# A planned hybrid-decoder step: freed buffers to the first in line, one group for linear outputs, split x, padded small products, a shorter Newton step

## The chip, the cores and the metric

The kernel runs on one core of one Trainium2 chip. The metric is the device time of one execution in microseconds (us); the median of three runs is the kernel's time. Engines are named as in the profile: PE (TensorE), DVE (VectorE), ACT (ScalarE), POOL (GpSimd) and SP (SyncE, which issues most DMAs).

## The reference

One layer of a decoder with two mixers side by side, for a prompt of 512 tokens and eight single new tokens of running sequences, with 1024 features.

```python
h = jnp.einsum('btd,de->bte', x, w_in)
qa, ka, va, za, ga, qb, kb, vb, gb = jnp.split(h, split_points, axis=-1)
log_a = log_sigmoid(za @ w_alpha2 + b_alpha) / GATE_TEMP
o_a, s_new = gla_chunked(qa, ka, va, log_a, s0, chunk)
o_a = o_a * rsqrt(mean(o_a ** 2) + RMS_EPS) * gla_norm_g
o_b = dilated_attention(qb, k_all, v_all, q_idx, rel_bias)
mix = concatenate([o_a * silu(ga), o_b * silu(gb)])
x_new = layer_norm(DEEPNORM_ALPHA * x + mix @ w_out, ln_g, ln_b)
```

Mixer a is gated linear attention (4 heads, a decayed state of 64 by 128 each); mixer b has 8 heads that look back in three strides with a bias table `rel_bias` of 32 buckets by 8 heads. The outputs are x_new for prompt and new tokens, the states, and new rows of keys and values.

## The kernel before, in words

**The products.** Tokens are columns: xT has 1024 rows in 8 k-tiles of 128 and 520 columns (256 prompt tokens, the 8 new ones, 256 prompt tokens), in two halves u of 264 and 256 columns (`TS`). Each float32 operand is split into a high part and a rest (`split`: ACT casts `hi`, DVE subtracts to get `lo`). Each product is three matmuls, high by high, weight's high by x's rest, weight's rest by x's high (`three` and `halves`). In the trace both parts of x are called `xx` and the weights `hi_ka`, `lo_ka` and so on.

**The order of the main products.** `dense()` is one generator that issues warm-up matmuls, then the input projection group by group: ka, the gate's low-rank product (`ps_za`, then `zT` on DVE and `ps_z`), qa, qb, kb, vb, gb, va, ga, and then the output projection (`ps_yf`, `ps_y`). For ka it goes over k-tiles as they arrive: for each k, each half u and each of two weight tiles, `three`. `first_loads` issues the DMAs of x and the ka weights in the order of the list FIRST, then constants, rel_bias into `rb_raw`, and adds `weight_loads`; `first_splits` splits what has landed and marks "xs" and "kas", for which `dense` waits with `At`.

**Around it** stand generators of the mixers. `scores` gives ps_s for a pair of heads and 128 queries; the softmax runs on DVE (`pr`, `ms`) and ACT; PE transposes `pr` into `ps_pt`, ACT casts it to `pth`, DVE takes the rest `ptl`; `weighted` multiplies into `ps_pv`. `gla_state` makes chunk states (`ps_kv`, `st_all`), `gla_out(u)` the outputs of two chunks in two banks (`ps_oa`): eight products of `att` by `va` with 128 rows, then products of the queries `qa` by a state with 64 rows. `gla_head` takes a chunk's outputs through the squares `sq`, `rmss` and the scaling of `oa`. `sample_softmax` handles logits of the new tokens (`ps_sl`, `ps_pn`), `sample_gla` their linear attention (`o_r`, `ps_ort`). `residual_sample` normalises the new tokens with two small products (`ps_ms`, `ps_vs`), and `norm(t)` a tile of 128 prompt tokens. `rsqrt` is Ln and Exp on ACT with a Newton step; with `between` (in `norm`) the whole step runs on ACT.

**What sets the order.** All generators are tasks of a `Plan` with a priority (small is first). A task yields an instruction (`Op`, or a `Batch` that is issued as one), a wish for a buffer (`Need`, several at once as `Pair`) or a mark to wait for (`At`). `Plan.run` repeats: it goes over the tasks in the order of priority, `advance`s each up to its next instruction, and chooses the one whose modelled start is earliest. Buffers are slots of fixed number per tag (`SLOTS`; PSUM banks in `BANKS`: d 3, s 3, t 2); `free` gives one back when its last share is given up. `dense` has the largest number, 100, so a buffer that both could take goes to others only if they are asked before it. Each engine's instruction list is fixed by this plan when the program is built. Every instruction that the plan issues carries the line of `issue`: L359.

Of the kernel before, what the change touches and what calls it, by code (L numbers as in the profile page):

```python
# [20 lines left out]
P = 128  # L21
# [3 lines left out]
NB = 8  # L25
# [23 lines left out]
C_W = 419  # L49
# [5 lines left out]

N_WARM = 8
# [133 lines left out]
class Plan:  # L190
# [173 lines left out]
def trunk(ctx: ExitStack, tc: tile.TileContext, xT, xp, xs, state, ck, cv, w_in, wab, gnorm,  # L364
# [23 lines left out]
    def rsqrt(o, x, scale, eps, between=None):  # L388
# [3 lines left out]
        yield V.tensor_scalar(x, x, scale, eps, op0=ALU.mult, op1=ALU.add)  # L392
        yield S.activation(o, x, AF.Ln)
        yield S.activation(o, o, AF.Exp, scale=-0.5)
        if between:

            add(between, 5)
            yield S.activation(t, o, AF.Square)
            yield S.mul(t, t, x)
            yield S.activation(t, t, AF.Copy, scale=-0.5, bias=1.5)  # L400
            yield S.mul(o, o, t)
        else:
            yield V.tensor_tensor(t, o, o, op=ALU.mult)
# [22 lines left out]
    rb = cst("rb", [66, NB, HB], F32R)  # L426
# [5 lines left out]
    q_s, k_s = cst("q_s", [P, 4, NB]), cst("k_s", [P, 4, NB])  # L432
    q_rows = cst("q_rows", [32, P])
    vnt, vat = cst("vnt", [P, 4, NB]), cst("vat", [P, 4, NB])
    lt = cst("lt", [P, 2, 64])
# [100 lines left out]
    def first_loads():  # L536
# [17 lines left out]
        B["rb_raw"] = yield Need("t1", "rb_raw", [64, NB, HB])  # L554
        for i in range(2):
            yield D.dma_start(B["rb_raw"][i * 32:i * 32 + 32], rel_bias[:, None, :].to_broadcast([32, NB, HB]))
# [6 lines left out]
    def first_splits():  # L563
        for j, (n, a, *b) in enumerate(FIRST):
            yield At("first", j + 1)
            if n == "x":
# [6 lines left out]
                yield from split(xraw[a // 2][:, a % 2, c], xh[a][:, c], xl[a][:, c])  # L573
                mark("xs")
# [106 lines left out]
    def dense():  # L681
# [9 lines left out]
        for k in range(KT):  # L691
            for u in range(2):
                yield At("kas", k + 1)
                yield At("xs", k + 1 + (u if k == 0 else 1))
                for i in range(2):
                    yield from three(pk[i, u][:, :TW[u]], k, halves(k, u, groups[f"ka{i}"]))
# [201 lines left out]
    def gla_state():  # L898
# [23 lines left out]
        plan.share(st, 3)  # L922
# [19 lines left out]
    def gla_queries():  # L942
# [12 lines left out]
        for h2 in range(2):  # L955
            plan.share(B[f"att{h2}"], 2)
        for u in range(2):
            yield from make(f"oa{u}", Need("g", f"oa{u}", [P, 2, 512]), 2)
            add(gla_out(u), 26 + u)

    def gla_out(u):

        yield At("st", 2 * u + 1)
        yield At("dg")
        va, att, qd = B[f"va{u}"], [B[f"att{h2}"] for h2 in range(2)], B["qa"]
        ps = yield Pair(*(bank("s", f"ps_oa{u}{h2}") for h2 in range(2)))
        po = {(h2, j, m): ps[h2][:, (2 * j + m) * P:(2 * j + m) * P + P] for h2 in range(2) for j in range(2) for m in range(2)}
        mm = Batch(T.matmul(po[h2, j, m], att[h2][:, (2 * u + j) * 2 + m, :], va[:, j, (m * 2 + h2) * P:(m * 2 + h2) * P + P],
                            start=j + m == 0, stop=False, skip_group_check=True) for h2 in range(2) for j in range(2) for m in range(2))
        mm += [T.matmul(po[h2, j, m], qd[h2 * 64:h2 * 64 + 64, m, (2 * u + j) * P:(2 * u + j) * P + P],  # L970
                        B["st"][h2 * 64:h2 * 64 + 64, 2 * u + j - 1, m, :], start=False, stop=j + m == 2, skip_group_check=True)
               for j in range(2) for m in range(2) for h2 in range(2) if u + j]
        yield mm
        free(qd, B["st"], *att)
        plan.share(va, 2)
        for h2 in range(2):
            plan.share(ps[h2], 2)
        for j in range(2):
            add(gla_head(u, j, ps, po), 26 + u + j / 2)
# [242 lines left out]
    def sample_logit(bi, past, qbc):  # L1222
# [4 lines left out]
        yield V.tensor_reduce(lt[:, :, bi * 8:bi * 8 + 8], past.rearrange("p k (h d) -> p k h d", d=64), axis=AX.X, op=ALU.add)  # L1227
# [3 lines left out]
    def sample_softmax():  # L1231
        yield At("kb", 8)
        yield At("lt", 5)
        sel = yield Need("t1", "sel", [64, C_AV - C_E2])
        yield D.dma_start(sel, c_f[:64, C_E2:C_AV])
        e2, pnm, m32 = sel[:, :P], sel[:, C_PN - C_E2:C_PN - C_E2 + 32], sel[:32, C_LN - C_E2:]
# [7 lines left out]
        l32 = yield Need("t1", "l32", [32, NB * HB])  # L1244
        yield V.tensor_reduce(ln_new, prod.rearrange("p (h d) -> p h d", d=64), axis=AX.X, op=ALU.add)
        free(prod)
        yield V.tensor_tensor(l32.rearrange("p (r u) -> p r u", u=2), ln_new[:, None, :].to_broadcast([32, 32, 2]),
# [9 lines left out]
        yield T.matmul(ps[:64, :258], rb.rearrange("p b h -> p (b h)"), cts, start=True, stop=False, skip_group_check=True)  # L1257
        yield T.matmul(ps[:64, 256:257], l32, one[:32], start=False, stop=False, skip_group_check=True)
        for k in range(2):
            yield T.matmul(ps[:64, k * P:k * P + P], lt[:, k, :], ident, start=False, stop=k == 1, skip_group_check=True)  # L1260
        free(cts, l32)
        mx_s, sum_s, pn_r = cst("mx_s", [64, 1]), cst("sum_s", [64, 1]), cst("pn_r", [64, 32])
# [8 lines left out]
        yield V.tensor_scalar(pn_r, pnm, p_s[:, 256:257], None, op0=ALU.mult)  # L1271
# [253 lines left out]
    def residual_sample():  # L1525
# [3 lines left out]
        avg = yield Need("t2", "avg", [64, 64])  # L1529
# [3 lines left out]
        yield D.dma_start(avg, c_f[:64, C_AV:])  # L1533
# [6 lines left out]
        sums, rstd = cst("sums_s", [64, 2]), cst("rstd_s", [64, 1])  # L1540
        yield V.tensor_reduce(sums[:, 0:1], y, axis=AX.X, op=ALU.add)
# [173 lines left out]
```

## Time and profile before

| | |
|---|---|
| median of three runs | 287.93 us (287.79 to 289.35) |
| the profiled execution | 288.67 us |
| its span | 286.8 us |
| PE busy | 275.0 us, 2636 instructions |
| DVE busy | 225.7 us, 547 instructions |
| ACT busy | 167.5 us, 478 instructions |
| POOL busy | 55.9 us, 74 instructions |
| DMA | 51.18 MB, mean 178 GB/s |

A row of the timeline gives start, duration, engine, line, operation, output from inputs, their shape and a count of equal instructions in a row; in brackets stands the idle time of the engine ahead of it and what ended it. PE overlaps matmuls, so the start of the next one tells more than the duration. A row of the windows gives the stretch, its length, busy time (and instructions) of PE, PEld (weight loads), DVE, ACT and POOL, the granted TensorE clock, the DMA engines' busy share and GB/s. The waits list who waited for whom: microseconds in total, times, and the longest.

### The profile page before, as it was taken

How to read it: one execution, taken by the hardware profiler on the slowest of the kernel's cores; microseconds unless marked ns; L12 is line 12 of the kernel's file. 1: busy time of each engine (PE TensorE's matmuls, PEld its weight loads, DVE VectorE, ACT ScalarE, POOL GpSimd, SP SyncE). 2: the span in 40 equal slices, each digit the busy share in tenths (PEclk: the TensorE clock that was granted, in tenths of full speed). 3: DMA queues.
4: the chain of work that ended last, by engine and by line, in shares of the span. 5: the costliest groups of instructions: out<-in, count | busy, mean ns of one | idle time of the engine just before them, and what ended most of it. 6: DMA issues, size and time to landing. Idle time of an engine off the chain costs nothing.

```text
span 286.8 us, 6896 instructions
## 1 busy us (share of the span) xinstructions
PE 275.0 (96%) x2636; PEld 259.5 (90%) x2636; DVE 225.7 (79%) x547; ACT 167.5 (58%) x478; POOL 55.9 (19%) x74
## 2 busy tenths in 40 slices
PE   8999999999999998999999999999999999999990
PEld 5899999998989998899989999999999999997880
DVE  3846897999889968988889997864888995339745
ACT  5757664554567777566869867526689774113201
POOL 4000001000782444401604444540000000000000
PEclk9999999999999999999999999999999999999997
DMA  7966522225866797648998987559754788741211
GB/s 209 269 191 195 147 75 75 75 78 167 296 201 222 196 287 230 175 130 243 274 201 188 239 227 219 149 149 228 221 95 148 230 297 252 111 151 73 78 75 73
DMA packets 58936, 51.18 MB, mean 178 GB/s; under 512 B 12555, under 2 KB 50197, under 8 KB 58903
## 3 DMA queue, kind: packets, MB, share of 16 engines
q1 hardware_dynamic: 58794, 50.66, 63.2%
q8 instruction: 21, 0.34, 0.5%
q14 instruction: 13, 0.10, 0.1%
q10 hardware_dynamic: 108, 0.07, 0.1%
HBM read 45.17 MB, written 6.03 MB: 179 GB/s over the span
## 4 chain that ended last, share of the span: by engine, by line
PE 71%; DVE 13%; DMA 8%; ACT 5%; issue 2%; SPq 1%; DVEq 0%; ACTq 0%
PE ps_qb L359 8%; PE ps_yf L359 8%; PE ps_y L359 8%; PE ps_ga L359 6%; PE ps_kb L359 4%; PE ps_qa L359 4%; PE ps_gb L359 4%; PE ps_va L359 4%; PE ps_ka L359 4%; DMA raw_gb__2152<-in_w_in_dram 3%; DMA out_dram<-feat 3%; PE ps_pt L359 2%; PE ps_va_f L359 2%; PE ps_l L359 2%; PE ps_s L359 2%; PE ps_pv L359 2%
## 5 line engine op out<-in xcount | busy, mean ns | idle before, releaser
L359 POOL TENSOR_TENSOR vv<-vv,pb 128x256 f32<-128x256 f32 x32 | 26.1, 846 | 45.5 <-DMA pb<-psd_s 39.8
L359 POOL TENSOR_TENSOR past<-past,qbc 128x256 f32<-128x256 f32 x32 | 25.6, 831 | 43.4 <-DMA past<-in_ck_dram 36.0
L359 ACT ACTIVATE pr<-pr,ms 128x128 f32<-128x128 f32 (+3 forms) x49 | 26.1, 546 | 5.8 <-DVE ms L359 5.2
L359 PE MATMUL ps_pt<-cf,pr 128*128 128x128 f32 x80 | 14.1, 280 | 1.4 <-DVE pt L359 1.0
L359 DVE CUSTOM_DVE_ANT_0 pr<-ps_s,strip 128x128 f32<-128x128 f32 (+3 forms) x32 | 14.3, 476 | 0.0
L359 PE MATMUL ps_ka<-xx,hi_ka 128*128 128x264 f32 (+1 forms) x64 | 13.5, 307 | 0.3 <-DVE xx L359 0.3
L359 ACT ACTIVATE sg<-sg 128x264 f32<-128x264 f32 (+1 forms) x32 | 13.4, 419 | 0.2
L359 PEld LDWEIGHTS ps_ka<-xx,hi_ka 128*128 128x128 f32 x64 | 11.0, 205 | 1.2 <-DVE xx L359 0.8
L359 DVE TENSOR_TENSOR ptl<-ps_pt,pth 128x384 fp32r<-128x384 f32 (+1 forms) x16 | 9.8, 617 | 2.8 <-ACT pth L359 2.8
L359 PEld LDWEIGHTS ps_pt<-cf,pr 128*128 128x128 f32 x80 | 9.0, 140 | 3.3 <-DVE pt L359 1.6
L359 ACT ACTIVATE d<-d 128x512 f32<-128x512 f32 x13 | 7.8, 637 | 6.7 <-DVE d L359 6.7
L359 ACT COPY feat_y<-ps_yf 128x256 f32<-128x256 f32 x8 | 3.0, 371 | 12.7 <-PE ps_yf L359 12.7
L359 ACT ACTIVATE rstd<-mv 128x1 f32<-128x1 f32 x4 | 0.7, 199 | 15.9 <-DVE mv L359 15.9
L359 POOL MEMSET att<- 64x512 f32 x2 | 1.0, 523 | 44.5 <-DVE ks L359 44.5
L359 ACT CAST pth<-ps_pt 128x384 fp32r<-128x384 f32 (+1 forms) x16 | 8.4, 534 | 2.2 <-PE ps_pt L359 2.0
L359 DVE TENSOR_REDUCE o_pv<-vv 128x4 f32<-128x1024 f32 x8 | 9.7, 1212 | 0.0
L359 DVE TENSOR_REDUCE lt<-past 128x16 f32<-128x1024 f32 x8 | 9.6, 1199 | 0.0
L359 PE MATMUL ps_ka<-xx,lo_ka 128*128 128x264 f32 (+1 forms) x32 | 9.4, 295 | 0.0
L359 DVE TENSOR_TENSOR obT<-ps_pv,pvl 64x256 f32<-64x256 f32 x16 | 6.6, 415 | 3.5 <-ACT pvl L359 3.3
L359 DVE TENSOR_TENSOR xx<-x_raw,xx 128x520 fp32r<-128x520 f32 (+2 forms) x9 | 5.8, 640 | 4.6 <-ACT xx L359 4.6
L359 ACT COPY pvl<-ps_pv 64x256 f32<-64x256 f32 x16 | 5.5, 370 | 6.1 <-PE ps_pv L359 5.3
L359 DVE TENSOR_TENSOR d<-b 128x1024 f32<-128x1024 f32 x7 | 8.5, 1218 | 0.0
(535 smaller groups left out, 1092.4 us busy)
## 6 DMA issues: line engine op xcount, KB each, us to landing
past<-in_ck_dram SPq DMA_DIRECT2D x8, 512.0 KB
vv<-in_cv_dram SPq DMA_DIRECT2D x8, 512.0 KB
pb<-psd_s SPq DMA_DIRECT2D x16, 256.0 KB
qbc<-qsd SPq DMA_DIRECT2D x8, 256.0 KB
strip<-tabr SPq DMA_DIRECT2D x8, 256.0 KB
y<-in_xp_dram SPq DMA_DIRECT2D x4, 512.0 KB
x_raw<-in_xT_dram SPq DMA_DIRECT2D x7, 260.0 KB
out_dram<-y SPq DMA_DIRECT2D x3, 512.0 KB
```

Of the source, the lines that this page charges most:

```text
L359: getattr(eng.eng, op.fn)(*op.args, **op.kw)
```

## The change

Five edits go together.

1. **The plan.** `free` notes that something was given back. `run` sorts the tasks once per step and goes through them from the front; as soon as an `advance` frees a slot, it begins again at the front, so that the first in line takes it. The choice by modelled start comes after.
2. **x.** k-tiles 0 to 2 (`N_HALF`) of x are split in the halves of `TS`, with a mark for each. In the ka products, high by high and weight's rest by x's high of both weight tiles come first, and the products with x's rest last.
3. **Linear outputs.** `gla_out` makes all four chunks at once, in four banks of the tags s or t, when all states are there: first all products with `att`, then all with states.
4. **Small products.** rel_bias is loaded into 128 columns instead of 64 (twice the copies, in pieces of 32 bytes), and the operands of `ps_sl`, `ps_pn`, `ps_ms` and `ps_vs` are padded to 128 rows and columns: `sel` and `avg` are loaded with 128 rows, `l32`, `pn_r` and `sums` are cleared with a memset, `q_s` and `k_s` lie in a third part of `lt`.
5. **The Newton step** in `norm`: eps and the factor -0.5 go into the DVE instruction ahead, Ln takes scale -2, and Copy takes x as its scale, so that one multiplication on ACT falls away.

The diff, cut to its core:

```diff
@@ free, run
             if self.shares[name] == 0:
+                self.freed = True
...
-            for t in sorted(self.tasks, key=lambda t: (t.prio, t.seq)):
-                if not self.advance(t):
+            line = sorted(self.tasks, key=lambda t: (t.prio, t.seq))
+            self.freed = True
+            while self.freed:
+                self.freed = False
+                for t in line:
+                    self.advance(t)
+                    if self.freed:
+                        break
+            for t in line:
+                if not t.heads:
                     continue
@@ rsqrt
         if between:
+            yield V.tensor_scalar(x, x, eps, -0.5, op0=ALU.add, op1=ALU.mult)
+            yield S.activation(o, x, AF.Ln, scale=-2.0)
+            yield S.activation(o, o, AF.Exp, scale=-0.5)
             add(between, 5)
             yield S.activation(t, o, AF.Square)
-            yield S.mul(t, t, x)
-            yield S.activation(t, t, AF.Copy, scale=-0.5, bias=1.5)
+            yield S.activation(t, t, AF.Copy, scale=x, bias=1.5)
             yield S.mul(o, o, t)
@@ first_loads, first_splits, dense
-        B["rb_raw"] = yield Need("t1", "rb_raw", [64, NB, HB])
+        B["rb_raw"] = yield Need("t1", "rb_raw", [64, 2 * NB, HB])
...
-                yield from split(xraw[a // 2][:, a % 2, c], xh[a][:, c], xl[a][:, c])
-                mark("xs")
+                for c in (c,) if b or a >= N_HALF else TS:
+                    yield from split(xraw[a // 2][:, a % 2, c], xh[a][:, c], xl[a][:, c])
+                    mark("xs")
...
-                for i in range(2):
-                    yield from three(pk[i, u][:, :TW[u]], k, halves(k, u, groups[f"ka{i}"]))
+                for last in (False, True):
+                    for i in range(2):
+                        pairs = halves(k, u, groups[f"ka{i}"])
+                        for j in (1,) if last else (0, 2):
+                            yield T.matmul(pk[i, u][:, :TW[u]], *pairs[j], start=k == 0 and j == 0, stop=k == KT - 1 and last)
@@ gla_out
-        yield At("st", 2 * u + 1)
+        yield At("st", 3)
...
-        ps = yield Pair(*(bank("s", f"ps_oa{u}{h2}") for h2 in range(2)))
+        banks = yield Pair(*(bank(("s", "t"), f"ps_oa{u}{h2}") for u in range(2) for h2 in range(2)))
@@ sample_softmax, residual_sample
-        yield T.matmul(ps[:64, 256:257], l32, one[:32], start=False, stop=False, skip_group_check=True)
+        yield T.matmul(ps[:, 256:257], l32, one, start=False, stop=False, skip_group_check=True)
...
-        yield T.matmul(ps[:64, 0:1], avg, sums[:, 0:1], start=True, stop=True)
+        yield T.matmul(ps[:, 0:1], avg, sums[:, 0:1], start=True, stop=True)
```

How the instructions then stand shows at three places. First PE at the start of the ka products. `xx0_105` (before) and `xx0_103` (after) are x's high parts, `xx0_106` and `xx0_104` the rests. Before:

```order
L359 MATMUL ps_ka00_122<-xx0_105,hi_ka0_132 128x264
L359 MATMUL ps_ka00_122<-xx0_106,hi_ka0_132 128x264
L359 MATMUL ps_ka00_122<-xx0_105,lo_ka0_133 128x264
L359 MATMUL ps_ka10_124<-xx0_105,hi_ka0_132 128x264
L359 MATMUL ps_ka10_124<-xx0_106,hi_ka0_132 128x264
L359 MATMUL ps_ka10_124<-xx0_105,lo_ka0_133 128x264
```

After:

```order
L371 MATMUL ps_ka00_120<-xx0_103,hi_ka0_130 128x264
L371 MATMUL ps_ka00_120<-xx0_103,lo_ka0_131 128x264
L371 MATMUL ps_ka10_122<-xx0_103,hi_ka0_130 128x264
L371 MATMUL ps_ka10_122<-xx0_103,lo_ka0_131 128x264
L371 MATMUL ps_ka00_120<-xx0_104,hi_ka0_130 128x264
L371 MATMUL ps_ka10_122<-xx0_104,hi_ka0_130 128x264
```

The two products with the rest have moved from places 2 and 5 to places 5 and 6.

Second, PE in the middle of the program, where the transposes of attention head 4 (`ps_pt42`, second half of the queries) stand among the products of the gate's third tile (`ps_gb2_0`). Before:

```order
L359 MATMUL ps_gb1_1_2360<-xx6_240,lo0_gb1__2139 128x256
L359 MATMUL ps_gb2_0_2470<-xx0_105,hi0_gb2__2149 128x264
L359 MATMUL ps_gb2_0_2470<-xx0_106,hi0_gb2__2149 128x264
L359 MATMUL ps_gb2_0_2470<-xx0_105,lo0_gb2__2150 128x264
...
L359 MATMUL ps_gb2_0_2470<-xx4_207,hi0_gb2__2149 128x264
L359 MATMUL ps_gb2_0_2470<-xx4_208,hi0_gb2__2149 128x264
L359 MATMUL ps_gb2_0_2470<-xx4_207,lo0_gb2__2150 128x264
L359 MATMUL ps_pt42_2490<-cf_66,pr42_2398 128x128 x3
```

After:

```order
L371 MATMUL ps_pv31_2454<-pth31_2328,vhl01_1581 128x128
L371 MATMUL ps_pv31_2454<-ptl31_2329,vhl01_1581 64x128
L371 MATMUL ps_gb2_0_2484<-xx0_103,hi0_gb2__2154 128x264
L371 MATMUL ps_gb2_0_2484<-xx0_104,hi0_gb2__2154 128x264
L371 MATMUL ps_gb2_0_2484<-xx0_103,lo0_gb2__2155 128x264
L371 MATMUL ps_pt42_2488<-cf_66,pr42_2419 128x128 x3
```

The transposes stand behind 3 products of this tile instead of 15.

Third, DVE at the same place, where `pr42` is head 4's softmax, `lo0_va0` a weight's rest and `ptl41` the rest of the transposed softmax. Before:

```order
L359 ISA pr52_2400,ms52_2422<-ps_s52_2404,strip51_2212 128x384
L359 ISA ms52_2422 128x1
L359 TENSOR_TENSOR obT11_2425<-ps_pv31_2433,pvl31_2463 64x256
L359 TENSOR_SCALAR pr42_2398<-pr42_2398,ms42_2420 128x384
L359 RECIPROCAL ms43_2421<-ms43_2421 128x1
```

After:

```order
L371 TENSOR_TENSOR lo0_va0__2462<-raw0_va0__2195,hi0_va0__2461 128x512
L371 RECIPROCAL ms42_2441<-ms42_2441 128x1
L371 ISA pr52_2421,ms52_2443<-ps_s52_2425,strip51_2220 128x384
L371 ISA ms52_2443 128x1
L371 TENSOR_SCALAR pr42_2419<-pr42_2419,ms42_2441 128x384
L371 TENSOR_TENSOR lo0_va0__2462<-raw0_va0__2195,hi0_va0__2461 128x512
```

Half of the weight's rest now stands ahead of the scaling of `pr42`, and one `obT` behind it. Every instruction of the changed kernel carries L371.

More of the change, by code (lines that the diff above doesn't have):

```diff
@@ L48 @@
 C_AV = 355
-C_W = 419
+C_W = 483
 T_P = 640
@@ L54 @@
 T_W = T_D + 258
+N_HALF = 3
 N_WARM = 8
@@ L431, in trunk @@
     ssq, rmss = cst("ssq", [P, TT * HA]), cst("rmss", [P, TT * HA])
-    q_s, k_s = cst("q_s", [P, 4, NB]), cst("k_s", [P, 4, NB])
     q_rows = cst("q_rows", [32, P])
     vnt, vat = cst("vnt", [P, 4, NB]), cst("vat", [P, 4, NB])
-    lt = cst("lt", [P, 2, 64])
+    lt = cst("lt", [P, 3, 64])
+    q_s, k_s = (lt[:, 2, i * 32:i * 32 + 32].rearrange("p (m b) -> p m b", b=NB) for i in range(2))
     o_pv, o_bs, o_as = cst("o_pv", [P, 4, NB]), vnt, cst("o_as", [P, NB * HA])
@@ L971, in gla_out @@
                         B["st"][h2 * 64:h2 * 64 + 64, 2 * u + j - 1, m, :], start=False, stop=j + m == 2, skip_group_check=True)
-               for j in range(2) for m in range(2) for h2 in range(2) if u + j]
+               for u in range(2) for j in range(2) for m in range(2) for h2 in range(2) if u + j]
         yield mm
         free(qd, B["st"], *att)
[L975 to L979, printed above, removed]
+        for u in range(2):
+            plan.share(B[f"va{u}"], 2)
+            ps = banks[2 * u:2 * u + 2]
+            for h2 in range(2):
+                plan.share(ps[h2], 2)
+            for j in range(2):
+                add(gla_head(u, j, ps, {k[1:]: x for k, x in po.items() if k[0] == u}), 26 + u + j / 2)
@@ L1528, in residual_sample @@
         w = yield Need("t2", "w_s", [64, 3, P])
-        avg = yield Need("t2", "avg", [64, 64])
+        avg = yield Need("t2", "avg", [P, P])
         yield D.dma_start(w[:, 0], by_tile(xs, KT))
```

74 lines of the change are left out of this document (39 added, 35 removed).

## The prediction

> **What bounds the kernel now.** I read the page's busy shares first, then the chain that ended last.
>
> ```profile
> PE 275.0 (96%) x2636; PEld 259.5 (90%) x2636; DVE 225.7 (79%) x547; ACT 167.5 (58%) x478; POOL 55.9 (19%) x74
> PE 71%; DVE 13%; DMA 8%; ACT 5%; issue 2%; SPq 1%; DVEq 0%; ACTq 0%
> ```
>
> PE is busy 275.0 of the 286.8 us, and holds 71% of the chain. So the time is PE's work, the small holes in it, a start and a tail. DVE, 79% busy over the whole, is the second engine. The waits of PE and windows of 10 us from the middle say where the two meet.
>
> ```profile
> PE ps_pt L359 <- DVE pt L359: 1.0, 3, 0.4
> PE ps_ka L359 <- DVE xx L359: 0.3, 1, 0.3
> ...
> PE ps_pt L359 <- DVE ptl L359: 0.3, 1, 0.3
> ...
> 140.00:150.00 10.00, 9.74 (x84) 8.97 (x83) 8.40 (x16) 7.03 (x16) 3.06 (x4) 1.00 1.00 242
> 150.00:160.00 10.00, 9.94 (x86) 9.76 (x85) 9.94 (x28) 8.67 (x24) 3.94 (x5) 1.00 0.92 202
> ```
>
> After the span, PE busy comes first here, then PEld, DVE, ACT. No recorded wait of PE is longer than 0.4, so an edit can win tenths, not microseconds, unless it takes PE work or tail away. From 150 to 160 PE and DVE are both full (9.94 of 10 each): whatever moves work of either there can make the other wait. The pace is 10 us for 86 matmuls, 0.116 each.
>
> The profiled execution took 288.67 (span 286.8 and 1.87 around it), 0.74 above the median of 287.93. I make the sum against 288.67 and carry the difference over to the median.
>
> **The start: x in halves, rests last.**
>
> ```profile
> 7.05 0.70 DVE L359 TENSOR_TENSOR xx<-x_raw,xx 128x520 fp32r<-128x520 f32 x1 [0.96 <-ACT xx L359]
> 9.76 0.70 DVE L359 TENSOR_TENSOR xx<-x_raw,xx 128x520 fp32r<-128x520 f32 x1 [0.29 <-ACT xx L359]
> ...
> 7.07 0.39 PE L359 MATMUL ps_ka<-xx,hi_ka 128*128 128x264 f32 x1
> 7.80 0.39 PE L359 MATMUL ps_ka<-xx,hi_ka 128*128 128x264 f32 x1 [0.34 <-DVE xx L359]
> 8.15 0.41 PE L359 MATMUL ps_ka<-xx,hi_ka 128*128 128x264 f32 x2
> 9.24 0.67 PE L359 MATMUL ps_ka<-xx,hi_ka 128*128 128x264 f32 x2
> ```
>
> The second matmul of k-tile 1 needs the rest of x, which DVE ends at 7.75. It starts 0.73 after the first, which at 0.12 a matmul is 0.61 lost. At 9.24 a pair takes 0.67 instead of 0.41, another 0.26. Now four matmuls on the high halves stand ahead of the rests (4 x 0.12 = 0.48), and a half of x is cast and subtracted in about half the time, so the rest is there some 0.35 earlier. Both holes should go: up to 0.87. The price is three more casts on ACT and three more subtractions on DVE with a fixed cost each, on engines that wait there anyway (0.96 and 0.29 in the rows). How much of it is passed on is read at the end of the phase.
>
> ```profile
> 17.11 1.05 ACT L359 CAST hi_qa__264<-raw_qa__174 128x1024 fp32r<-128x1024 f32 x1 [1.81 <-DMA raw_qa__174<-in_w_in_dram]
> 18.27 1.15 DVE L359 TENSOR_TENSOR lo_qa__265<-raw_qa__174,hi_qa__264 128x1024 fp32r<-128x1024 f32 x1
> 18.23 2.05 PE L359 MATMUL ps_za<-x_raw,zw 128*32 128x128 f32 x64
> 20.35 0.60 DVE L359 TENSOR_SCALAR zT<-ps_za,one 128x128 f32<-128x128 f32 x2 [0.93 <-PE ps_za L359]
> ```
>
> ps_za would start and end earlier, but zT stands on DVE behind lo_qa, which ends at 19.42 because raw_qa lands at 17.1. zT waits 0.93 for ps_za now, so an earlier ps_za is covered up to about that. But the padding doubles the copies of rel_bias (pieces of 32 bytes, 512 of them now), which SP issues ahead of raw_qa.
>
> ```profile
> 13.00:14.00 1.00, 1.00 (x11) 1.00 (x10) 0.97 (x3) 0.63 (x2) 0.00 (x0) 1.00 0.81 67
> ...
> 15.00:17.00 2.00, 2.00 (x19) 2.00 (x18) 0.74 (x3) 0.25 (x1) 0.00 (x0) 1.00 1.10 322
> ```
>
> Of these windows the last two columns count: from 13 to 14 the DMA engines are 0.81 busy and move 67 GB/s, with raw_qa's large pieces from 15 to 17 it is 322. So small pieces hold the engines for about 0.8 us. If the doubling costs as much again, raw_qa lands and lo_qa ends 0.8 later, at 20.2, and zT starts there instead of 20.35: 0.15 gained. From 14 to 15 they have room, though, which may take the new pieces up. Ends: 0.87 or 0.15; I take 0.5.
>
> The Trainium skill, DMA: Bandwidth & Descriptors, Specifications, gives 512 B as the least transfer for full rate, with a read-modify-write below it. The low rate from 13 to 14 agrees; by that rule the new pieces cost as much as the old, which is rival D.
>
> **Small products padded to the whole array.**
>
> ```profile
> 123.47 0.28 PE L359 MATMUL ps_sl<-cts,rb 66*64 66x258 f32 x1
> ...
> 123.88 0.65 PE L359 MATMUL ps_sl<-cf,lt 128*64 128x128 f32 x4
> 124.46 0.79 PE L359 MATMUL ps_pv<-pt,vhl 128*128 128x256 f32 x5
> ...
> 259.98 0.27 PE L359 MATMUL ps_ms<-sums_s,avg 64*64 64x1 f32 x2
> 260.18 0.50 PE L359 MATMUL ps_y<-hi_wo__3464,mla 128*128 128x512 f32 x1
> 260.52 0.40 PE L359 MATMUL ps_y<-hi_wo__3525,mha 128*128 128x512 f32 x1
> ...
> 257.26 2.79 PE ps_y L359 x12
> ```
>
> Around ps_ms (a 64*64 piece of the array) the next matmul takes 260.18 to 260.52 = 0.34, against 2.79/12 = 0.23 in a plain run: 0.11 for changing the shape back. Changing into it I put at the same, about 0.1, so 0.2 goes for ps_ms and 0.2 for ps_vs if a padded pass costs the 0.10 that it has now (260.18 - 259.98 for two). ps_sl takes 123.47 to 124.46 = 0.99 for seven passes; at 0.12 for the long one, 0.10 for two of one column and 0.11 for four of 128 it would be 0.76, so 0.23. ps_pn moves out of a group of 64 rows to between matmuls of vb, with two passes of its own and a memset ahead: -0.1. Sum 0.5; ends 0.2 (the padded pass costs more than 0.10) and 0.8 (a change of shape costs 0.2 each way). The memsets and the larger sel are off the path: they come microseconds ahead of their readers; without that cover a memset would cost some 0.2, like the smallest rows here.
>
> **Linear outputs in one group.**
>
> ```profile
> 202.69 0.71 PE L359 MATMUL ps_oa<-st_all,qa 64*128 64x128 f32 x8
> 203.34 0.39 PE L359 MATMUL ps_ga<-xx,lo_ga__2975 128*128 128x264 f32 x1
> ...
> 207.95 1.16 PE L359 MATMUL ps_oa<-st_all,qa 64*128 64x128 f32 x16
> 209.04 0.51 PE L359 MATMUL ps_ga<-xx,hi_ga__2974 128*128 128x256 f32 x2
> ...
> 204.03 0.31 ACT L359 ACTIVATE sq<-oa 128x128 f32<-128x128 f32 x1 [2.02 <-DVE oa L359]
> ...
> 208.12 0.40 ACT L359 ACTIVATE oa<-oa,rmss 128x128 f32<-128x128 f32 x1 [0.24 <-DVE rmss L359]
> ...
> 209.52 0.31 ACT L359 ACTIVATE sq<-oa 128x128 f32<-128x128 f32 x1 [0.67 <-DVE oa L359]
> ...
> 223.65 0.40 ACT L359 ACTIVATE oa<-oa,rmss 128x128 f32<-128x128 f32 x1 [0.30 <-DVE rmss L359]
> ...
> 227.71 0.33 PE L359 MATMUL ps_ort<-cf,o_r 128*128 128x128 f32 x1 [0.30 <-DVE o_r L359]
> ```
>
> Eight state passes take 0.65 and sixteen 1.09 from start to next start: 0.055 a pass and 0.21 for the change of shape. Leaving it adds about the 0.11 seen at ps_ms. One group instead of two saves one such pair, 0.32. Against it, the first heads start later: the group's passes for u=1 now come ahead of them, the sixteen state passes' 0.9 and, where they don't fill the wait for the last states, sixteen att passes of some 0.12: about 2 us in all. ACT has idled 2.02 for oa when the first head reaches it, so this delay goes straight into its chain, which runs through the heads to o_r; ps_ort already waits 0.30 for that at 227.71. On the way ACT has holes of 0.24, 0.67 and 0.30, which take 1.2 of the 2.0. Passed on to PE: 0, if other ga matmuls go ahead in those twenty microseconds, to 0.8; I take 0.
>
> **Newton in one step less.**
>
> ```profile
> 281.74 0.21 ACT newton L359
> 281.95 0.02 issue
> ```
>
> In the tail nothing runs beside the norm of the last tile, and the removed step with its issue is 0.21 + 0.02 = 0.23, all on the path.
>
> **Who gets what is freed; the middle.** The largest move is between 130 and 180: the transposes of the second half's softmax come forward. ps_pt of head 4 stands behind 3 matmuls of gb2 instead of 15, and all ps_pt and ps_pv of this half now stand ahead of va.
>
> ```profile
> 144.23 0.56 DVE L359 TENSOR_TENSOR ptl<-ps_pt,pth 128x384 fp32r<-128x384 f32 x1 [1.22 <-ACT pth L359]
> 152.88 0.52 DVE L359 TENSOR_SCALAR pr<-pr,ms 128x384 f32<-128x384 f32 x1
> 153.54 0.52 PE L359 MATMUL ps_pt<-cf,pr 128*128 128x128 f32 x3
> ```
>
> DVE ends head 4's weights at 153.40 and PE starts their transposes at 153.54: they are already just in time. Twelve matmuls fewer ahead are 12 x 0.12 = 1.4 us, and DVE gets one more half of lo_va ahead of that row, less one obT: 0.2. At DVE's present pace PE waits about 1.5 to 2.0 there. DVE can't hurry, since it is full; but its list changes too (some copies go to ACT, and lo_va and o_pv stand later), and ahead of it lies a hole of 1.22 at 144.23, pinned by the landing of raw_gb. From below: the holes that PE has in the middle now (0.3 for ptl, two or three of the 1.0 for pt, some 1.1 together) all vanish. From above: 2.0 here and 1 to 1.5 at the later heads, 3.5, less the 1.1 saved. Between -1.1 and +2.4 I take +0.6, nearer the middle because what PE loses early it doesn't wait for late.
>
> **The sum.** -0.5 (start) -0.5 (products) -0.32 (group) -0.23 (tail) +0.6 (middle) = -0.95: 288.67 becomes 287.7, and the median 287.93 becomes 287.0.
>
> **Rivals.** B: the new order of DVE's work fits, and the middle loses its holes: -1.55 - 1.1 = -2.65, so 285.3. For it speaks that all softmax rows stand earlier on DVE as well as on PE; against it, the full DVE from 150 to 160.
>
> C, the other side: PE stands at the transposes of heads 4 to 7 because DVE is not done with their weights. Lost are 2.0 at head 4 and 1.5 at the later ones, won the 1.55 of the other edits: +1.95, so 289.9. The kernel gets slower than it is once these waits sum to more than 1.55. For it speaks the 0.14 between DVE's end and PE's start above; against it, that the work which DVE puts off here is work for which PE needn't wait later.
>
> D: the small pieces eat the start's gain (0.15 left, not 0.5), and the later heads pass their 0.8 on to ps_ort: -0.15 - 0.5 - 0.32 - 0.23 + 0.6 + 0.8 = +0.2, so 288.1. It would look as if the change did nothing. For it, zT's place behind lo_qa and ACT's 2.02; against it, the room from 14 to 15.
>
> **How the numbers follow.** Forecast 0.45, B 0.23, C 0.18, D 0.14. Half a per cent is 1.44 us, about what a measurement of this kernel can tell from no change: faster is below 286.5, slower above 289.4. The forecast's own range is 286.0 to 288.0, from the ends of the start (0.4 either way), the small products (0.3) and a few tenths of the middle; about 0.13 of its 0.45 lies below 286.5. With B that makes 0.36 for faster. C gives 0.13 to slower, and what I don't see in the others 0.04: 0.17. Same is the rest, 0.47. The range takes in B and C with half a microsecond below the one and up to the price of the other: 284.8 to 290.0.
>
> **What would show it.** Right: no hole over 0.2 between PE's matmuls from 7 to 10 and ps_za starting 0.6 or more earlier; zT waiting for ps_za still; rows of ps_ms and ps_vs with the next ps_y at 0.23; one group of ps_oa; the tail's ACT chain one row of newton shorter; PE's waits for pt at 130 to 180 summing to 1.5 to 2. Wrong: a wait of over 1.8 at head 4's ps_pt (C), none there (B), zT waiting for lo_qa or ps_ort for over 1 (D). A time below 284.8 would mean that PE did less work than I count, or ran denser where I see no hole.

## The result, and the profile after

The changed kernel takes 292.24 us (median of 6 runs, 291.63 to 293.11), the kernel before 288.62 beside it (6 runs, 287.79 to 289.35): a ratio of 1.0113 with a 95% interval of 1.0084 to 1.0143, so 3.3 us slower. The forecast was 287.0, with 290.0 as its upper end. The profiled execution of the changed kernel took 292.23 with a span of 290.4, 3.6 more than before. The page of its profile:

```profile
PE 275.3 (95%) x2636; PEld 260.4 (90%) x2636; DVE 225.7 (78%) x553; ACT 167.7 (58%) x475; POOL 54.9 (19%) x74
...
PE 56%; DVE 22%; DMA 10%; ACT 7%; issue 2%; SPq 2%; DVEq 0%; ACTq 0%
```

PE's busy time is the same within 0.3 (275.0 before). What grew is the time in which it has nothing to do, and in the chain that ended last DVE goes from 13% to 22% and DMA from 8% to 10%. The waits of PE:

```profile
PE ps_gb L371 <- DVE ms L371: 1.6, 1, 1.6
...
PE ps_ort L371 <- DVE o_r L371: 1.0, 1, 1.0
PE ps_tab L371 <- DVE tsb L371: 0.9, 1, 0.9
...
PE ps_qa L371 <- DVE lo_qa__271 L371: 0.5, 1, 0.5
```

None of these four was there with more than 0.3 before. (The longest one of before in the body of the program is not among the waits that the prediction shows: 0.6 of a product of vb for the rest of its weights, so its "No recorded wait of PE is longer than 0.4" is wrong. It is there in the changed kernel too, with 0.6, and explains nothing of the loss.)

```profile
PE ps_vb_f L359 <- DVE lo_vb__1820 L359: 0.6, 1, 0.6
```

The four new waits lie at three places. To see what each costs, I take the same instruction in both timelines and how much later it starts:

| PE's instruction | before | after | later |
|---|---|---|---|
| last of ps_ka | 18.02 | 17.60 | -0.42 |
| last of ps_qa | 32.70 | 34.11 | +1.42 |
| last of ps_vb | 130.58 | 131.51 | +0.93 |
| last of ps_va | 196.17 | 198.95 | +2.79 |
| last of ps_yf | 255.50 | 259.67 | +4.17 |
| last of ps_y | 278.98 | 282.79 | +3.80 |
| end of DVE's last instruction | 286.77 | 290.33 | +3.56 |

So from ps_ka to ps_qa 1.84 are lost after 0.42 won; 0.49 come back by 131; 1.86 are lost in the middle and 1.38 from there to 256; 0.37 and 0.24 come back at the end.

**The start.** One row of DVE in the kernel before (L359), then rows of ACT, DVE and PE in the changed kernel (L371):

```profile
17.79 0.42 DVE L359 CAST ct<-ct_raw 66x512 fp32r<-66x512 f32 x1 [1.98 <-DMA ct_raw<-in_c_t_dram]
...
19.45 1.04 ACT L371 CAST hi_qa__270<-raw_qa__179 128x1024 fp32r<-128x1024 f32 x1 [3.79 <-DMA raw_qa__179<-in_w_in_dram]
...
20.16 0.42 DVE L371 CAST ct<-ct_raw 66x512 fp32r<-66x512 f32 x1 [4.00 <-DMA ct_raw<-in_c_t_dram]
...
20.64 1.15 DVE L371 TENSOR_TENSOR lo_qa__271<-raw_qa__179,hi_qa__270 128x1024 fp32r<-128x1024 f32 x1
21.72 0.58 DVE L371 TENSOR_SCALAR zT<-ps_za,one 128x128 f32<-128x128 f32 x2
...
20.73 0.39 PE L371 MATMUL ps_tab<-ct,rb 66*8 66x512 f32 x1 [0.87 <-DVE tsb L371]
...
21.85 0.40 PE L371 MATMUL ps_qa<-xx,lo_qa__271 128*128 128x264 f32 x1 [0.48 <-DVE lo_qa__271 L371]
```

The two holes of the ka products are gone; a smaller one has come at 8.87, where PE waits 0.15 for ACT's cast of x, and ka ends 0.42 earlier, not the 0.87 of the two holes. But raw_qa lands at 19.45 instead of 17.11 and the bias table's input at 20.16 instead of 17.79. lo_qa ends at 21.79, and zT, which waited 0.93 for ps_za before, now stands behind lo_qa with no idle time ahead of it. The windows:

```profile
13.00:14.00 1.00, 1.00 (x10) 1.00 (x10) 0.97 (x3) 0.64 (x2) 0.00 (x0) 1.00 1.16 103
14.00:15.00 1.00, 1.00 (x11) 1.00 (x10) 0.67 (x2) 0.63 (x1) 0.00 (x0) 1.00 0.39 35
15.00:16.00 1.00, 1.00 (x11) 1.00 (x10) 0.74 (x2) 0.30 (x1) 0.00 (x0) 1.00 0.56 133
```

Two microseconds go by at 103 and 35 GB/s, and the large pieces begin 0.84 later (raw_qa's first piece of 512 bytes starts at 15.15 instead of 14.31).

**The middle.** PE and DVE ahead of the transposes of head 4:

```profile
151.70 0.22 PE L371 MATMUL ps_pv<-ptl,vhl 128*64 128x128 f32 x1
153.49 0.51 PE L371 MATMUL ps_gb<-xx,hi_gb__2154 128*128 128x264 f32 x2 [1.56 <-DVE ms L371]
...
153.97 0.27 PE L371 MATMUL ps_pt<-cf,pr 128*128 128x128 f32 x1
...
152.22 0.68 DVE L371 TENSOR_TENSOR lo_va__2462<-raw_va__2195,hi_va__2461 128x512 fp32r<-128x512 f32 x1
...
152.90 0.53 DVE L371 CUSTOM_DVE_ANT_0 pr<-ps_s,strip 128x384 f32<-128x384 f32 x1
153.36 0.07 DVE L371 DVE_READ_ACCUMULATOR2_ANT ms<- 128x1 f32 x1
```

The same product and the same read in the kernel before:

```profile
151.51 0.40 PE L359 MATMUL ps_gb<-xx,hi_gb__2149 128*128 128x264 f32 x2
...
151.86 0.53 DVE L359 CUSTOM_DVE_ANT_0 pr<-ps_s,strip 128x384 f32<-128x384 f32 x1
```

The product that waits is a main one, the first of a gate tile, not a transpose. By the profile's releaser it needs a PSUM bank from which DVE still reads a head's scores (152.90 to 153.43), and DVE has put half of lo_va ahead of that read. In the kernel before, the same product began at 151.51, ahead of the same read at 151.86, so there it had another bank. Head 4's transposes, three products later, then find their weights ready.

**The linear outputs and the tail.**

```profile
206.53 1.17 PE L371 MATMUL ps_oa<-va,att 128*128 128x128 f32 x9
207.63 1.61 PE L371 MATMUL ps_oa<-st_all,qa 64*128 64x128 f32 x24
209.17 0.40 PE L371 MATMUL ps_ga<-xx,lo_ga__2974 128*128 128x264 f32 x1
...
208.75 0.31 ACT L371 ACTIVATE sq<-oa 128x128 f32<-128x128 f32 x1 [4.08 <-DVE oa L371]
...
232.22 0.33 PE L371 MATMUL ps_ort<-cf,o_r 128*128 128x128 f32 x1 [0.96 <-DVE o_r L371]
```

The group's state passes take 207.63 to 209.17 = 1.54, as worked out (24 x 0.055 + 0.21 = 1.53). But ACT has idled 4.08 when the first head comes, not 2.02, and starts on it at 208.75 instead of 204.03, 4.7 later, where PE was 2.8 behind (the end of va). The wait at ps_ort went from 0.30 to 0.96. In the tail one newton row is missing, and from the end of PE's products to DVE's last y it is 283.10 to 285.86 = 2.76 instead of 3.00.

### The profile page after: what moved, and what is told of

The parts are those of the page before. It is cut to its first block, busy times and chain, and to the rows that moved or that the text cites. A ratio compares the mean times of both kernels' runs of the same rounds, so it can differ in the third digit from the quotient of the medians.

```text
span 290.4 us, 6901 instructions
## 1 busy us (share of the span) xinstructions
PE 275.3 (95%) x2636; PEld 260.4 (90%) x2636; DVE 225.7 (78%) x553; ACT 167.7 (58%) x475; POOL 54.9 (19%) x74
## 4 chain that ended last, share of the span: by engine, by line
PE 56%; DVE 22%; DMA 10%; ACT 7%; issue 2%; SPq 2%; DVEq 0%; ACTq 0%
PE ps_qb L371 8%; PE ps_yf L371 8%; PE ps_y L371 8%; PE ps_gb L371 4%; PE ps_qa L371 4%; PE ps_va L371 4%; PE ps_va_f L371 4%; DVE pr L371 3%; DMA out_dram<-feat 3%; PE ps_l L371 2%; PE ps_vb L371 2%; DMA ct_raw<-in_c_t_dram 2%; DMA x_raw<-in_xT_dram 2%; PE ps_pv L371 2%; PE ps_s L371 2%
## 5 line engine op out<-in xcount | busy, mean ns | idle before, releaser
L371 POOL TENSOR_TENSOR vv<-vv,pb 128x256 f32<-128x256 f32 x32 | 25.4, 825 | 48.0 <-DMA pb<-psd_s 39.0
L371 POOL TENSOR_TENSOR past<-past,qbc 128x256 f32<-128x256 f32 x32 | 25.2, 820 | 43.5 <-DMA past<-in_ck_dram 38.6
L371 ACT ACTIVATE pr<-pr,ms 128x128 f32<-128x128 f32 (+3 forms) x48 | 25.3, 543 | 4.3 <-DVE ms L371 3.9
L371 PE MATMUL ps_pt<-cf,pr 128*128 128x128 f32 x80 | 13.9, 277 | 0.4 <-DVE pt L371 0.3
L371 DVE CUSTOM_DVE_ANT_0 pr<-ps_s,strip 128x128 f32<-128x128 f32 (+3 forms) x32 | 14.2, 475 | 0.0
L371 PE MATMUL ps_ka<-xx,hi_ka 128*128 128x264 f32 (+1 forms) x64 | 13.4, 306 | 0.2 <-ACT xx L371 0.2
L371 ACT ACTIVATE sg<-sg 128x264 f32<-128x264 f32 (+1 forms) x32 | 13.4, 417 | 0.3
L371 ACT ACTIVATE d<-d 128x512 f32<-128x512 f32 x13 | 7.8, 636 | 6.7 <-DVE d L371 6.7
L371 PEld LDWEIGHTS ps_ka<-xx,hi_ka 128*128 128x128 f32 x64 | 10.9, 206 | 0.7 <-ACT xx L371 0.4
L371 DVE TENSOR_TENSOR ptl<-ps_pt,pth 128x384 fp32r<-128x384 f32 (+1 forms) x16 | 9.7, 616 | 1.8 <-ACT pth L371 1.7
L371 ACT COPY feat_y<-ps_yf 128x256 f32<-128x256 f32 x8 | 3.0, 372 | 13.4 <-PE ps_yf L371 13.4
L371 PEld LDWEIGHTS ps_pt<-cf,pr 128*128 128x128 f32 x80 | 9.3, 140 | 1.5 <-DVE pt L371 0.8
L371 DVE TENSOR_REDUCE o_pv<-vv 128x4 f32<-128x1024 f32 x8 | 9.7, 1213 | 0.6 <-POOL vv L371 0.6
L371 ACT ACTIVATE rstd<-mv 128x1 f32<-128x1 f32 x4 | 0.7, 199 | 15.7 <-DVE mv L371 15.7
L371 POOL MEMSET att<- 64x512 f32 x2 | 1.0, 523 | 45.9 <-DVE ks L371 45.9
L371 DVE TENSOR_REDUCE lt<-past 128x16 f32<-128x1024 f32 x8 | 9.6, 1202 | 0.0
L371 ACT CAST pth<-ps_pt 128x384 fp32r<-128x384 f32 (+1 forms) x16 | 8.2, 532 | 1.6 <-PE ps_pt L371 1.4
L371 PE MATMUL ps_ka<-xx,lo_ka 128*128 128x264 f32 (+1 forms) x32 | 8.9, 298 | 0.0
L371 DVE TENSOR_TENSOR d<-b 128x1024 f32<-128x1024 f32 x7 | 8.5, 1217 | 0.0
L371 DVE TENSOR_TENSOR obT<-ps_pv,pvl 64x256 f32<-64x256 f32 x16 | 6.6, 414 | 2.4 <-ACT pvl L371 2.2
L371 PE MATMUL ps_s<-kp,qh 64*128 64x128 f32 (+3 forms) x64 | 8.3, 344 | 0.0
L371 DVE TENSOR_TENSOR xx<-x_raw,xx 128x520 fp32r<-128x520 f32 (+2 forms) x11 | 5.9, 551 | 2.8 <-ACT xx L371 2.5
```

Of the source, the lines that this page charges most:

```text
L371: getattr(eng.eng, op.fn)(*op.args, **op.kw)
```

## Experiments

Twelve kernels ran, four to a chip, each beside the kernel before on the same chip. Executions there spread by some 1.5 us to either side, so a ratio's interval (95%, against the kernel before) decides on time, and a profile tells where one execution lost it. The changed kernel has two ratios to compare with, 1.0113 and, on another chip, 1.0135. Theory 1 was at first: each edit has its own place and price, and they add up.

**The old way of handing out what is freed**, the rest changed:

```diff
-            line = sorted(self.tasks, key=lambda t: (t.prio, t.seq))
...
+            for t in sorted(self.tasks, key=lambda t: (t.prio, t.seq)):
+                if not self.advance(t):
                     continue
```

> The changed kernel with the old way of handing out what is freed (the other four edits stay). Theory 1 (each edit has its own place and price, and they add up): the wait of 1.7 us at the first product of the gate's third tile goes, the middle from 132 to 198 us costs as much as in the kernel before, and the time is 292.2 - 1.9 = 290.3. Theory 2 (in the middle DVE or DMA sets the pace whatever the order is): the wait comes back at other places of the middle, and the time stays within 0.5 of 292.2.

Measured: 1.0074 (1.0038 to 1.011). That is 1.1 to 1.8 us better than the changed kernel, with intervals that overlap, and it doesn't tell the theories apart: without the plan's edit the order in the middle is not that of before either. From 24 to 200 us it is the one that padding the softmax products makes alone (below). Its profiled execution was the slowest of nine (295.76, median 291.73), and its waits are not used.

**rel_bias loaded once per row**, the rest changed:

```diff
-        B["rb_raw"] = yield Need("t1", "rb_raw", [64, 2 * NB, HB])
+        B["rb_raw"] = yield Need("t1", "rb_raw", [64, HB])
...
-            yield D.dma_start(B["rb_raw"][i * 32:i * 32 + 32], rel_bias[:, None, :].to_broadcast([32, 2 * NB, HB]))
+            yield D.dma_start(B["rb_raw"][i * 32:i * 32 + 32], rel_bias)
...
+        wide = raw[:, None, :].to_broadcast([64, 2 * NB, HB])
+        yield S.copy(rb[:64], wide)
```

> The changed kernel, with rel_bias loaded once per row (64 pieces of 32 bytes instead of 1024) and spread to the 128 columns by the ACT cast; PE's order is unchanged. Theory 1: the first weights of qa land about 2.5 us earlier, at 17 us or before, the waits of ps_tab and ps_qa on DVE (0.9 and 0.5) go, ps_qa ends 1.8 earlier, and the gain is carried to the end: 290.4. Theory 2 (the middle is set by DVE and DMA): the first 40 us gain 1.8, but the wait in the middle grows by as much, and the time stays within 0.5 of 292.2. Theory 3 (it is the split of x, not the copies, that makes SP's list late): the weights land less than 0.5 earlier.

Measured: 1.0082 (1.0047 to 1.0116), 0.9 to 1.5 us better than the changed kernel with intervals that overlap; span 289.0. ACT and DVE at the start:

```profile
16.05 1.05 ACT L371 CAST hi_qa__270<-raw_qa__179 128x1024 fp32r<-128x1024 f32 x1 [1.07 <-DMA raw_qa__179<-in_w_in_dram]
...
19.49 0.60 DVE L371 TENSOR_SCALAR zT<-ps_za,one 128x128 f32<-128x128 f32 x2 [1.08 <-PE ps_za L371]
```

raw_qa lands 3.4 earlier, zT waits for PE again, and ps_qa ends at 31.86, 2.25 ahead of the changed kernel. At the end of vb (130.00) 1.5 of that are left, at the end of this execution 1.4. So theory 3 falls, theory 1 holds for the start, and a third of the gain is lost on the way, before the middle. The middle itself still loses 2.1 (from 0.58 ahead of before at the end of vb to 1.55 behind at the end of va).

**The plan's edit alone**, on the kernel before (the lines of `free` and `run` of the diff above, nothing else):

> The kernel before with only the new way of handing out what is freed. Theory 1: nothing moves ahead of 117 us, the middle loses 1.9 to a wait of a product on a PSUM bank or of a transpose on DVE: 288.6 + 1.9 = 290.5. Theory 2: within 0.5 of 288.6.

Measured: 1.0025 (0.9994 to 1.0057), span 288.6. The middle loses 0.6 there and the stretch to 256 another 0.6, with a wait of 0.6 of a va product for DVE's `ms`. Theory 1 in its first form falls: the interval ends at 1.65 us, so the plan's edit has no price of 1.9 of its own.

**The linear outputs in two groups again**, the rest changed (`gla_out(u)` as before):

> The changed kernel with the linear outputs in two groups again, as before; nothing moves ahead of 203 us. Theory 1: the heads of the first half start some 3 us earlier, the wait of 1.0 at ps_ort shrinks below 0.4, the second change of shape costs 0.3 back: 292.2 - 0.6 = 291.6. Rival (the chain to ps_ort hangs on the linear attention of the new tokens, not on the heads): the wait at ps_ort stays at 1.0 and the time is 292.5.

Measured: 1.0043 (1.0013 to 1.0072). ps_ort waits 0.3. Against 1.0113 and 1.0135 for the changed kernel (below) that is 2.0 and 2.7 us better, three to four times the 0.6 that I had expected of it. The rival (the wait at ps_ort stays) falls.

**The changed kernel again**, as the measure on the chip of the next three:

> The changed kernel itself, on the chip of the next three, as their measure. All theories: 1.011 of the kernel before (3.3 us more), ps_qa ending 1.4 late and the wait of PE for DVE in the gate's third tile.

Measured: 1.0135 (1.0096 to 1.0174), and in its profile the same row as above:

```profile
PE ps_gb L371 <- DVE ms L371: 2.6, 2, 1.6
```

**x split and its rests last, alone**, on the kernel before (the edits in `first_splits` and `dense`):

> The kernel before with only x split in halves and its rests last; PE's order differs in nothing behind the ka products. Theory 1 (each edit has its place and its price): ka ends 0.4 to 0.6 earlier, ps_qa and all behind it too, since raw_qa isn't later: 0.5 us faster. Theory 3 (the split makes SP's list late): raw_qa lands late, ps_qa ends 1 us late, and the kernel is 1 us slower.

Measured: 1.0003 (0.9967 to 1.0038), so nothing that can be told from no change. In its profile raw_qa lands in time and ps_qa ends 0.29 earlier:

```profile
17.03 1.05 ACT L360 CAST hi_qa__272<-raw_qa__181 128x1024 fp32r<-128x1024 f32 x1 [1.68 <-DMA raw_qa__181<-in_w_in_dram]
```

That execution then lost 1.3 in one wait for `pt` near 113, which the order didn't cause: there it is that of before. Theory 3 falls a second time; the gain of 0.3 is below what the spread lets one see.

**A selection**: x as above, rel_bias once per row, ps_ms and ps_vs padded, the shorter Newton step; ps_sl, ps_pn, the plan and the linear outputs as before:

> The kernel before with x split and its rests last, rel_bias loaded once per row (64 pieces of 32 bytes), the two products of the new tokens' norm padded, and the shorter Newton step; the order of PE between 120 and 255 us is that of before. Theory 1: start -0.9, norm products -0.4, tail -0.2: 1.5 us faster than before, no wait over 0.6 in the middle. Theory 2 (DVE or DMA sets the middle): the 0.9 of the start is gone by 196 us, and the kernel is 0.5 faster.

Measured: 0.9947 (0.9917 to 0.9977), so 1.5 us faster than before. It is the only version that beats both kernels. The waits of its profile:

```profile
PE ps_pt L360 <- DVE ptl L360: 0.9, 1, 0.9
PE ps_vb_f L360 <- DVE lo_vb__1824 L360: 0.7, 1, 0.7
PE ps_pt L360 <- DVE pt L360: 0.6, 2, 0.4
```

The profiled execution, one of its slower ones (288.46 where the median is 287.64), was 0.84 ahead at the end of vb and 0.07 ahead at the end of va, with one wait of 0.9 in the middle against theory 1's 0.6. The times agree with theory 1, the profile more with theory 2; this is not settled.

**The softmax products padded, alone**, on the kernel before (the edits in `sample_softmax`, `rb` and `lt`):

> The kernel before with only the products of the new tokens' softmax padded (rel_bias in twice the pieces, ps_sl and ps_pn on the whole array), under the old plan. It moves PE's order in the middle as well (191 of 540 products there have another neighbour). Theory 1, as it stands now (what costs in the middle is any order which the plan makes anew, since its modelled times miss the DVE by microseconds): ps_qa ends 1.5 late by the pieces, and the middle loses 1 to 3 more by waits of PE on DVE: 2.5 to 4.5 slower. Rival (it takes the new way of handing out what is freed to lose in the middle): 1.5 slower, all of it at the start.

Measured: 1.0127 (1.0071 to 1.0183), as much as the whole change, with the old plan. The start is not the cause: raw_qa lands at 17.41, 0.3 late, and ps_qa ends 0.08 late. The middle is:

```profile
169.60 0.52 PE L359 MATMUL ps_va_f<-xx,hi_va__2458 128*128 128x264 f32 x2 [1.91 <-DVE ms L359]
```

It is the same kind of wait as in the changed kernel, a main product for a bank from which a head's scores are read. The profiled execution was the fastest of its six (290.34; the others go up to 294.5).

**The same with rel_bias once per row:**

> As the kernel with only the softmax products padded, and with rel_bias loaded once per row: the same instructions in the same order, without the small pieces. Theory 1 (the order in the middle is what costs): the start gains 0.3 to 0.7, the middle still loses 1.5, and the kernel is 2.5 to 3.5 slower than before instead of 3.7. Rival (the pieces of rel_bias cost it all): no slower than before, within 0.7.

Measured: 1.0088 (1.0059 to 1.0117), 2.5 us slower. Without the small pieces raw_qa lands at 16.70 and ps_qa ends 0.18 ahead of before, but the loss is mostly still there, and so is its wait:

```profile
170.16 0.62 PE L359 MATMUL ps_va_f<-xx,hi_va__2458 128*128 128x264 f32 x2 [2.45 <-DVE ms L359]
```

The rival (the pieces cost it all) falls.

**The linear outputs in one group, alone**, on the kernel before:

> The kernel before with only the linear outputs in one group; nothing moves ahead of 200 us. Theory 1 (the heads start late and ACT and DVE pass it on): the second change of shape saves 0.3, the wait at ps_ort grows from 0.3 to 1 or more: 0.5 to 1 slower. Rival (as forecast): 0.3 faster, ps_ort waits as before.

Measured: 1.0066 (1.0039 to 1.0093), 1.9 us slower. In the profile PE is 2.3 behind already when ga begins (a part that this edit doesn't touch, so it is that execution's own), and 4.2 at PE's last product: 1.9 lost behind ga's start.

```profile
218.82 0.39 PE L359 MATMUL ps_ga<-xx,hi_ga__3123 128*128 128x264 f32 x1 [1.12 <-DVE ga L359]
...
215.82 0.88 DVE L359 TENSOR_SCALAR oa<-oa,rmss 128x128 f32<-128x128 f32 x4
216.62 1.22 DVE L359 TENSOR_TENSOR lo_ga__3325<-raw_ga__3126,hi_ga__3324 128x1024 fp32r<-128x1024 f32 x1
217.75 0.68 DVE L359 TENSOR_TENSOR lo_wo__3350<-raw_wo__3147,hi_wo__3349 128x512 fp32r<-128x512 f32 x1
218.35 0.41 DVE L359 TENSOR_TENSOR ga<-ps_ga,sg 128x256 f32<-128x256 f32 x1
```

The outputs of all four chunks come at once; DVE works off four `oa` and two weight rests, and only then empties the bank that PE waits for.

**One number of the plan's model, twice**, on the kernel before. No edit adds or takes away work. PE's instructions are the same in another order. On ACT and DVE the expectations' "every instruction is the same" is not quite so: the plan also chooses which of the two does a copy or a scaling, and by the traces 14 of these change engine in the first run and 16 in the second.

```diff
-SWITCH = 230.0
+SWITCH = 250.0
```

> The kernel before with one number of the plan's model changed, the cost of a change of shape on PE from 230 to 250 ns. Every instruction is the same; only the order differs, at 148 of 540 places of the middle and at 94 of 600 behind it. Theory 1 (an order that the plan makes anew loses waits of PE for DVE, whatever made it new): 1 to 3 us slower than before. Rival (the order as such is worth nothing, the loss comes from what the edits add): within 0.7 of before.

Measured: 1.0069 (1.0039 to 1.0098). Its largest wait:

```profile
234.28 0.30 PE L359 MATMUL ps_ort<-cf,o_r 128*128 128x128 f32 x1 [1.94 <-DVE o_r L359]
```

```diff
-TO_PE, FROM_PE, OTHER, AFTER_DMA, WITHIN = 600.0, 250.0, 150.0, 500.0, 120.0
+TO_PE, FROM_PE, OTHER, AFTER_DMA, WITHIN = 580.0, 250.0, 150.0, 500.0, 120.0
```

> The kernel before with another number of the plan's model changed, the delay from another engine to PE from 600 to 580 ns; every instruction is the same, the order differs at 197 of 540 places of the middle. Theory 1: 1 to 3 us slower than before. Rival: within 0.7.

Measured: 1.0203 (1.0174 to 1.0233), 5.9 us slower, twice as bad as theory 1 said at most. Its profile loses most behind ga, not in the middle:

```profile
240.79 0.39 PE L359 MATMUL ps_yf<-mhb,hi_wo__3705 128*128 128x264 f32 x1 [1.86 <-ACT hi_wo__3705 L359]
```

Two plans that nobody chose, with the same work, cost 0.7% and 2.0%. So that a new order, with the choice of ACT or DVE that comes with it, can cost as much as the whole change is shown. In which wait it is lost differs from order to order.

**All profiles side by side.** PE's order in the middle is one of four, made by the plan's edit and by the softmax products' padding; the other edits leave it alone. The time from the last product of vb to the last of va, one profiled execution each (that of the slowest execution above left out):

| order in the middle | runs | us |
|---|---|---|
| of before | before, x alone, selection, one group alone | 65.59, 66.13, 66.36, 66.79 |
| plan's edit alone | plan alone | 66.18 |
| padding alone | padding alone, the same with rel_bias once | 67.07, 69.43 |
| both | changed kernel (twice), rel_bias once, two groups | 67.44, 68.34, 67.72, 68.77 |

With the softmax products padded each profile is slower there than each without, by 0.3 to 3.8. With the plan's edit alone it is not. The two runs with one number changed, with orders of their own, have 64.89 and 67.01 and lose more behind ga.

## Why the prediction was wrong

In the two profiles the change costs 3.56 where 0.95 was to be won. Of the 4.51 between them the start has 1.92, the middle 1.26 and the group of linear outputs 1.70 (from va to the end of yf). The small products, with the stretches that they stand in, came 0.36 better, the tail as put.

**The start** was put at 0.5 gained between ends of 0.87 and 0.15, and lost 1.42. Its gain was mis-sized: 0.42 at the end of ka, in part because PE now waits for ACT's cast of x at 8.87. The step that failed is "if the doubling costs as much again, raw_qa lands and lo_qa ends 0.8 later". It landed 2.3 later (17.11 to 19.45). Rival D had the place and the wrong price, because it took the delay of the first piece for the delay of the last: SP issued raw_qa 0.84 later (13.27 to 14.11) and its first piece came 0.84 later, but the landing 2.34. Shown is that neither edit does it alone: raw_qa lands at 17.03 with x split, at 17.41 with the pieces doubled, and at 19.13 to 19.45 in three profiles with both. The forecast priced them one by one.

The packets in the traces say where the other 1.5 lie. In every profile one packet of 16 KB from the instruction queue (q8 on the page) comes by between 16.0 and 17.3 and takes 0.9 to 1.2 us (0.93 in the changed kernel, at 16.77). Without both edits (ten profiles) it comes when at least 57 of the 66 pieces of the table's input, which stands behind raw_qa in SP's list, have started, and these 66 follow each other without a gap above 0.08. With both edits (all four profiles, that of the slowest execution above among them) it comes before the first of them, in the midst of raw_qa's pieces; then 60 pieces come in a row and the last six 0.5 to 1.2 later. So the 0.84 let the instructions' load get in among raw_qa's pieces, and a small share of both loads is late. That this share stood behind the 16 KB on one DMA engine is argued: which packet ran on which engine is not recorded.

The Trainium skill, DMA: Bandwidth & Descriptors, Specifications, gives 512 B as the least transfer for full rate. The runs agree in direction only: doubled alone, the 32-byte pieces delay raw_qa by 0.3, and without them it lands 3.4 earlier in the changed kernel. Rival D, for which that rule spoke, was given 0.14.

**The small products** were put at 0.5 and gained about that. ps_sl:

```profile
124.20 0.29 PE L371 MATMUL ps_sl<-cts,rb 66*128 66x258 f32 x1
124.33 0.28 PE L371 MATMUL ps_sl<-cf,l 128*128 128x1 f32 x2
124.47 0.48 PE L371 MATMUL ps_vb<-hi_vb__1821,xx 128*128 128x256 f32 x2
124.79 0.60 PE L371 MATMUL ps_sl<-cf,lt 128*128 128x128 f32 x4
125.15 0.85 PE L371 MATMUL ps_pv<-pt,vhl 128*128 128x256 f32 x6
...
264.05 0.28 PE L371 MATMUL ps_ms<-sums_s,avg 128*128 128x1 f32 x2
264.19 0.48 PE L371 MATMUL ps_y<-hi_wo__3475,mla 128*128 128x512 f32 x1
264.51 0.39 PE L371 MATMUL ps_y<-hi_wo__3534,mha 128*128 128x512 f32 x1
```

ps_sl's own parts are 0.27 and 0.36 = 0.63 instead of 0.99; the two products of vb between them take 0.32, some 0.08 more than in a plain run. At ps_ms two passes take 0.14 instead of 0.20, but the product behind it still takes 0.32. The step "0.11 for changing the shape back" was wrong; that the term's size came out near is in part luck, since the padded passes took 0.07 each where 0.10 was put. What the term left out is that these edits make the plan write a new order: the softmax products' padding alone is 1.0127.

**One group** was put at 0.32 gained and 0 passed on. The first part is right (one change of shape is gone, and the state passes take 1.54 as worked out); the step that failed is "0, if other ga matmuls go ahead in those twenty microseconds, to 0.8; I take 0". Alone the edit costs 1.9, and undoing it saves 2.0 to 2.7. I had asked whether PE has other products meanwhile. It has, but alone the edit makes one of them wait 1.12 for its bank, which DVE empties behind the outputs of the chunks. In the changed kernel itself the recorded wait is the one that rival D named, ps_ort for o_r, 0.96 instead of 0.30, that is 0.66 where D had put 0.8. With the 0.32 saved, 1.70 were lost from va to the end of yf; beyond these 0.66 their place is open.

**The tail** was put at 0.23 and gave 0.24.

**The middle** was put at +0.6 between -1.1 and +2.4, and cost 1.86. That lies inside the term's ends; what failed is the wait that it was made of ("PE waits about 1.5 to 2.0 there", at head 4's transposes). Rival C had the place, heads 4 to 7, but not the price, 3.5 lost where 1.86 were, and not the wait: the transposes didn't wait, but a main product did, for a bank. That the wait of 1.56 falls into the forecast's 1.5 to 2.0 is luck. C was given 0.18, as one of several that exclude each other. Losses at the places of C and of D came together, and with them the change is slower. Their chances should not have excluded each other.

Behind the middle stands one assumption: that the order made anew is as good as the old but for the places that were priced. The two runs with one number changed show that it need not be. Theory 1 had to be changed for it. The start's loss belongs to two edits together, and the group's loss to one. The middle's loss came in with the softmax products' padding, also under the old plan, and not with the plan's edit, to which the forecast had given it. That the padding costs by the order which it makes the plan write, and not by the little that it adds (two memsets, wider operands), is argued: ps_sl itself got shorter, and the waits are those of main products for banks.

## What to carry to other kernels

Where a planner writes the order, an edit's price is its own plus that of a new order. Compare the new order with a few that are as arbitrary. Keep edits that leave the order alone apart from those that don't: here the split of x, rel_bias once per row, the norm's products and the Newton step together give 0.5%. Look for the banks as well as the data: a main product that takes a buffer from a slower engine waits for all that stands ahead of the read on that engine's list. When two edits delay the same transfer, price them together, and ask what else reaches the DMA engines in the time by which it is late.

## What the runs showed that I had not expected

The product behind a small one takes 0.32 instead of 0.23 also when the small one has the whole array (264.19 to 264.51), so that part of the cost is not the change of shape; what the padding saves at ps_ms is 0.08 ahead of it (0.32 to 0.24), 0.03 a pass and 0.02 behind it. And executions of one program spread by more than the change is worth: 287.35 to 291.48 for the kernel with x alone, so that a single profile can be off by 2 us without any edit at the place (2.3 at the start of ga with one group alone).
